# A fused encoder layer on one core: weight tiles 4608 bytes apart, norm tiles at the upper end of SBUF

## The chip, the cores and the metric

The kernel runs on one core of a Trainium2 chip. The metric is device time in microseconds (us) from one launch to its end. The kernel before took 1044.92 us (median of three runs, 1043.6 to 1045.78). One further execution was recorded by the hardware profiler; its rows are quoted below.

## The reference, cut to what matters

One layer of a streaming encoder on 1024 tokens of width 1024, float32 throughout:

```python
hn = _rmsnorm(h, norm_mix_g)
proj = einsum('bsd,de->bse', hn, w_in)          # 1024 x 2564 columns
# four token mixers on column groups: pooling, spatial gating, short convolution, Mamba-2 SSD
mix = concatenate([y_a, y_b, y_c, y_d], axis=-1)
h = h + einsum('bse,ed->bsd', mix, w_out)
hn = _rmsnorm(h, norm_ffn_g)
gate = silu(einsum('bsd,df->bsf', hn, w_gate))  # d_ff = 2816
up = einsum('bsd,df->bsf', hn, w_up)
h = h + einsum('bsf,fd->bsd', gate * up, w_down)
return _rmsnorm(h, final_norm_g)
```

## The kernel before

All arrays lie with 128 features (or 128 tokens) on the partitions. Every long product is taken in three matmuls: each operand `a` is split into a rounded part `hi` and a rest `lo` (`split`, L97 on ScalarE and L98 on VectorE; L101 and L102 where it is scaled as well), and `mm3` (L90 to L92) adds `hi*hi`, `hi*lo` and `lo*hi` in one PSUM bank. Each matmul is preceded by its own weight load, which in the profile runs on its own row (PEld) beside the matmul before it. The moving operand of nearly all of them is 512 columns of 4 bytes, that is 2048 bytes of each partition; the stationary one is 128 columns, 512 bytes.

The stages, in order of time:

- **Input projection and mixers (to about 276 us).** `proj_T` (L271) makes 14 tiles of 128 output features. For each of eight `k` it runs `hi*xh`, `hi*xl` and `lo*xh`, each for two halves of the tokens: six matmuls of 512 columns, 48 a tile, 672 in all. Stationary are the weight tiles `wh_t`/`wl_t` of the pool `whl`, moving the activations `x_hi`/`x_lo` of the pool `hl`. `proj_N` makes the z, u and v columns with the roles exchanged (256 or 260 columns moving). Between them run the short float32 matmuls of the state-space mixer and of the gating.
- **Output projection (to about 360 us).** `project`: 16 groups of 24 matmuls, stationary `oh`/`ol`, moving `mix_hi`/`mix_lo`.
- **First FFN block (to about 426 us).** `plain`: eight groups of 24.
- **Ten FFN chunks (426 to 1003 us).** Each runs `strassen` twice, for `w_gate` and `w_up`: seven products of 12 matmuls each (four `kt` by three). Stationary are the weight pairs `wg_i`/`wu_i` (pools `rfa` and `rf`, three slots in turn), moving the seven activation sets T[1] to T[7] (`t1h`, `t2h`, `t3h`, `t_hi`). Into their order the generator `down` puts the down projection of the chunk before: 84 matmuls a chunk, stationary `dh`/`dl`, moving the gated activations `x_ih`/`x_il`. So a chunk has 168 + 84 = 252 matmuls of 512 columns. VectorE makes all `lo` halves, adds the Strassen parts in PSUM to the sums (L734) and adds the down products to `h1` (L814).
- **Last block and final norm (from 1003 us).**

Where the tiles lie: pools take SBUF from its lower end upwards in the order in which they are opened, those with `side="right"` from its upper end downwards; a tile takes its bytes rounded up to 32. Offsets below are byte addresses in a partition, modulo 512:

| tiles | offset before |
|---|---|
| `hl` (x, mix and the sets T[4] to T[7]), `ext` (T[1], T[2]) | 0 |
| `wh`/`wl` of the input stage, slots 0 to 3 | wh 128, wl 256; wh 384, wl 0; the same again |
| `oh`/`ol`, FFN weight pairs, `t3h`/`t3l`, `x_ih`/`x_il`, `dh`/`dl` | 384 |
| working tiles `m` of `sml` (`g`, `u`, `xt`) | 96 |
| `wTs`, `pw`, `xbc`, `E`, `xb`, `xd` (short float32 products) | 128 |
| `rB`, `vnt`, `yzt`, `tri` | 0 |

The weight slots of the input stage are 1056 words of 4 bytes, 4224 bytes, apart, which is 8 times 512 and 128.

[...]

Of the kernel before, what the change touches and what calls it, by code (L numbers as in the profile page):

```python
# [9 lines left out]
F32 = mybir.dt.float32  # L10
# [5 lines left out]
P = 128  # L16
# [3 lines left out]
NB = S // P  # L20
# [3 lines left out]
NP = NF // 2 - 1  # L24
EPS = 1e-6
WK = 1040
WT = 1056
NH = 4


# [8 lines left out]
NPAR = C_INV + 32  # L39

R_LG, R_LB, R_DTB, R_ALOG, R_D = 0, 256, 512, 516, 520
NROW = 524
# [3 lines left out]
def encoder_kernel(ctx, tc, xT, w_t, w_z, w_vd, w_u, pool_w, sgu_wT, par, row, w_out, w_gate, w_up, w_dp, w_dl, gfin, out):  # L46
# [6 lines left out]
    acts = ctx.enter_context(tc.tile_pool(name="acts", bufs=8))  # L53


    const.tile([P, 8], F32, name="pad_left")
    padr = ctx.enter_context(tc.tile_pool(name="padr", bufs=1, side="right"))
    padr.tile([P, 24], F32, name="pad_right")

    gffn = const.tile([P, NK], F32, name="gffn")  # L60
    ident = const.tile([P, P], F32, name="ident")
# [9 lines left out]
    def rsqrt(pool, x, n, tag):  # L71

        y = pool.tile([P, n], F32, name=f"rs_y_{tag}", tag="rs_y", bufs=2)
        t = pool.tile([P, n], F32, name=f"rs_t_{tag}", tag="rs_t", bufs=2)
        yi, xi = y.bitcast(I32), x.bitcast(I32)
        V.tensor_scalar(out=yi, in0=xi, scalar1=1, scalar2=None, op0=ALU.arith_shift_right)
        V.tensor_scalar(out=yi, in0=yi, scalar1=-1.0, scalar2=float(0x5F3759DF), op0=ALU.mult, op1=ALU.add)
        for _ in range(3):
            V.tensor_tensor(out=t, in0=y, in1=y, op=ALU.mult)
            V.scalar_tensor_tensor(out=t, in0=t, scalar=-0.5, in1=x, op0=ALU.mult, op1=ALU.mult)  # L80
            V.scalar_tensor_tensor(out=y, in0=t, scalar=1.5, in1=y, op0=ALU.add, op1=ALU.mult)
        return y
# [27 lines left out]
    def inv_rms(pool, psp, tag, qs, name):  # L110

        n = qs[0].shape[1] // P
        ps = psp.tile([P, 512], F32, name=f"ps_ss_{name}", tag=tag)
        for b in range(n):
            for i, q in enumerate(qs):
                nc.tensor.matmul(ps[:, b:b + 1], q[:, b * P:(b + 1) * P], ones,
                                 start=(i == 0), stop=(i == len(qs) - 1))
        ms = pool.tile([P, n], F32, name=f"ms_{name}", tag="ms", bufs=2)
        V.tensor_scalar(out=ms, in0=ps[:, :n], scalar1=1.0 / D, scalar2=EPS, op0=ALU.mult, op1=ALU.add)
        return rsqrt(pool, ms, n, name)  # L120

    def rows_by_dma(pool, psp, tag, rn, n, out, name, rt=None, bufs=1):

        pt = psp.tile([P, 512], F32, name=f"ps_rt_{name}", tag=tag)
        nc.tensor.transpose(pt[0:n, 0:P], rn, ident)
        t = pool.tile([n, P], F32, name=f"rt_{name}", tag=rt or f"rt{n}", bufs=bufs)
        V.tensor_copy(out=t, in_=pt[0:n, 0:P])
        dr = tc.dram_tile([1, n * P], F32, name=f"rd_{name}")
        nc.sync.dma_start(out=dr.rearrange("o (b s) -> (o b) s", b=n), in_=t)
        nc.sync.dma_start(out=out, in_=dr.to_broadcast([P, n * P]))  # L130
# [21 lines left out]
    h1 = [None] * 8  # L152
# [22 lines left out]
    with ExitStack() as a:  # L175
        bt = a.enter_context(tc.tile_pool(name="bt", bufs=1, reuse_waits="tile"))
        sb = a.enter_context(tc.tile_pool(name="sb", bufs=1, reuse_waits="tile"))
# [3 lines left out]
        psm = a.enter_context(tc.tile_pool(name="psm", bufs=5, space=PSUM, reuse_waits="tile"))  # L181
        pss = a.enter_context(tc.tile_pool(name="pss", bufs=3, space=PSUM, reuse_waits="tile"))

        sb.tile([P, 16], F32, name="pad_sb")
        part = bt.tile([P, 128], F32, name="part")[:, :NPAR]
        nc.sync.dma_start(out=part, in_=par)

        def pc(c):
# [4 lines left out]
        def w_tiles(n, name):  # L193
            slot = next(loads) % 4
            raw = wraw.tile([P, WK], F32, name=f"wr_{name}", tag="wraw")[:, :n]
            hi = whl.tile([P, WT], F32R, name=f"wh_{name}", tag=f"whi{slot}")[:, :n]
            lo = whl.tile([P, WT], F32R, name=f"wl_{name}", tag=f"wlo{slot}")[:, :n]
            return raw, hi, lo
# [10 lines left out]
        rB = bt.tile([P, S], F32, name="rB")  # L209
# [10 lines left out]
        qa = [rB, yzt[:, 0:4, :].rearrange("p b c -> p (b c)")]  # L220
# [22 lines left out]
        for k in range(NK):  # L243
            x = mix[k]
# [3 lines left out]
                (V if k % 2 else nc.gpsimd).tensor_tensor(out=qa[k % 2], in0=qa[k % 2], in1=q, op=ALU.add)  # L248

        nc.gpsimd.tensor_copy(out=gffn, in_=part[:, C_GFFN:C_GFFN + NK])  # L250
        rowt = bt.tile([P, 544], F32, name="rowt")[:, :NROW]
        nc.sync.dma_start(out=rowt, in_=row.to_broadcast([P, NROW]))
        wTs = bt.tile([P, NH, P], F32, name="wTs")
        nc.sync.dma_start(out=wTs, in_=sgu_wT)
# [60 lines left out]
        rn = inv_rms(sb, pss, "sm", qa[:1], "x")  # L315
        for b in range(NB):
            ps = pv[b] if b < 2 else proj_N(wv, 260, b, "v", *((pss, "sm") if b % 2 else ()))
            if b == 3:
                rows_by_dma(sb, pss, "sm", rn, NB, rB, "x")
            V.scalar_tensor_tensor(out=dt[:, b, :], in0=ps[:, 256:260], scalar=rn[:, b:b + 1],  # L320
                                   in1=rowt[:, R_DTB:R_DTB + 4], op0=ALU.mult, op1=ALU.add)
            nc.scalar.mul(out=vn[b], in_=ps[:, :256], mul=rn[:, b:b + 1])
            st = sb.tile([P, 6], F32, name=f"st{b}", tag="st", bufs=2)
            V.bn_stats(out=st, in_=vn[b])
            V.bn_aggr(out=mv[:, b, :], in_=st)
# [67 lines left out]
        ss = sb.tile([P, NB * 2], F32, name="ss")  # L393
# [179 lines left out]

    ext = ctx.enter_context(tc.tile_pool(name="ext", bufs=1, reuse_waits="tile"))
    sml = ctx.enter_context(tc.tile_pool(name="sml", bufs=1, reuse_waits="tile"))
    sml.tile([P, 24], F32, name="pad_sml")
    NM = 6
    rfa = ctx.enter_context(tc.tile_pool(name="rfa", bufs=1, reuse_waits="tile"))
    fp = ctx.enter_context(tc.tile_pool(name="fp", bufs=8, space=PSUM, reuse_waits="tile"))
# [61 lines left out]
    with tc.tile_pool(name="ror", bufs=2, side="right", reuse_waits="tile") as ror, \  # L641
            tc.tile_pool(name="roh", bufs=1, side="right", reuse_waits="tile") as roh, \
            tc.tile_pool(name="ro", bufs=1, side="right", reuse_waits="tile") as ro, \
            tc.tile_pool(name="rol", bufs=1, side="right", reuse_waits="tile") as rol:
        wo, qa = {}, []

        def load_out(d):
            raw = ror.tile([P, S], F32, name=f"or{d}", tag="raw")
            nc.sync.dma_start(out=raw, in_=w_out[d])
            wo[d] = [(rol if d < 2 else roh if d < 4 else ro).tile([P, S], F32R, name=f"o{n}{d}") for n in "hl"]  # L650
            split(raw, *wo[d])

        w0 = {}
        pairs = [(w, i, j) for w, i in ((w_gate, 0), (w_up, 0), (w_gate, 1), (w_up, 1)) for j in range(2)]

        def first_w(m):
            w, i, j = pairs[m]
            src = ror.tile([P, S], F32, name=f"r0{m}", tag="raw")[:, :HS]
            nc.sync.dma_start(out=src, in_=w[i][:, j * HS:(j + 1) * HS])
            w0[m // 2, j] = w_pair(src, f"w0{m}")  # L660

        for th in range(2):
            qa.append(sums(f"h{th}"))
            for n in range(8):
                d = (n + 2 * th) % 8
                if th == 0 and n >= 2:
                    load_out(d)
                    residual(d)
                if th or n >= 2:
                    project(fp, "b", d, th, wo[d])  # L670
                last_add = squares(sml, d, n, th * HS, HS, qa[th])
                if th == 0 and n < 4:
                    mix_split(2 * n, 1)
                    mix_split(2 * n + 1, 1)
                if th == 0 and n >= 6:
                    load_out(n - 6)
                if th == 1 and n in (3, 4):
                    first_w(n - 3)
                if th == 1 and n == 1:
                    V.tensor_tensor(out=qa[0][0], in0=qa[0][0], in1=qa[0][1], op=ALU.add)  # L680
                    rn2 = inv_rms(sml, fp, "b", qa[0][:1], "h0")
                if th == 1 and n == 2:
                    rms_rows(rows_diag(sml, fp, "b", rn2, 4, "h0", "m", NM)[0], 0)
                    T[1], T[2] = t_set(0, "t1"), t_set(1, "t2")
                    for i in (1, 2):
                        for j in range(4):
                            t = sml.tile([P, HS], F32, name=f"n{i}{j}", tag="m", bufs=NM)
                            normed(4 * (i - 1) + j, 0, t)
                            split(t, *T[i][j])
# [174 lines left out]
    rn2 = []  # L864
    T[3], T[5], T[6] = t_set(2, "t3"), t_set(4, "t5"), t_set(5, "t6")

    def half_rms():
        follow(V.tensor_tensor(out=qa[1][0], in0=qa[1][0], in1=qa[1][1], op=ALU.add), last_add)
        rn2.append(inv_rms(sml, fp, "b", qa[1][:1], "h1"))

    rx2 = []

# [78 lines left out]
    for q in range(2):  # L951
        for i in range(2):
            wd[i, q] = w_pair(raw_tile(w_dl[i, :, q * HS:(q + 1) * HS], f"rl{i}{q}"), f"wl{i}{q}", tag=f"g{4 + 2 * i + q}" if i + q < 2 else None)
    ss = sml.tile([P, NB + 1], F32, name="ssf")
    ms = sml.tile([P, NB], F32, name="msf")
    LAST = NB - 1

    def square(b, c, to):
# [106 lines left out]
```

## Time and profile before

| | |
|---|---|
| median of three runs | 1044.92 us |
| the profiled execution, its own time | 1043.13 us |
| its span (first to last instruction) | 1041.4 us |
| PE (matmul) | 1019.9 us busy, 4836 instructions |
| PEld (weight loads) | 840.2 us |
| DVE (VectorE) | 828.7 us |
| ACT (ScalarE) | 399.2 us |
| POOL (GpSimd) | 293.2 us |
| granted TensorE clock, mean | 0.997 |

Matmuls overlap in the records: each one of 512 columns is shown for about 0.39 to 0.40 us, but the next one starts some 0.23 us after it. So the busy share of PE tells little, and the distance from one start to the next tells what a matmul costs. The timeline gives starts to 0.01 us; over ten or more matmuls that is 1 ns each.

### The profile page before, as it was taken

To read this page: it belongs to the slowest core of one execution; us is meant where nothing else is said; L and a number is where in the kernel's file an instruction comes from. 1 tells how busy PE (TensorE), PEld (TensorE's weight loads), DVE (VectorE), ACT (ScalarE), POOL (GpSimd) and SP (SyncE) were. 2 spreads that over 40 slices of the span, in tenths; PEclk is the share of its full clock that TensorE was granted. 3 is DMA by queue.
4 is the path that set the end of the run, shared out by engine and by line. 5 is a ranking of instruction groups with operands and counts; after the bars stand their busy time and mean duration, and the time that the engine had idled before them with its cause. 6 is when DMAs were issued, how large, how long until landed. Compare 5 with 4: busy or idle time off the path is not lost.

```text
span 1041.4 us, 13299 instructions
## 1 busy us (share of the span) xinstructions
PE 1019.9 (98%) x4836; PEld 840.2 (81%) x4836; DVE 828.7 (80%) x1375; ACT 399.2 (38%) x730; POOL 293.2 (28%) x325
## 2 busy tenths in 40 slices
PE   6999999999999999999999999999999999999997
PEld 5987998888887778888787878788787878788785
DVE  6698345887752689979898998979898898979777
ACT  8155412132440344434333343334333343434353
POOL 4014000000010140243444334443444334443302
PEclk9999999999999999999999999999999999999999
DMA  7311012111540201121111111121111111211203
GB/s 267 102 61 62 21 52 65 51 48 52 162 141 1 82 11 41 51 61 52 59 47 56 42 61 52 61 61 51 60 44 59 41 61 51 61 62 50 68 5 161
DMA packets 29682, 67.61 MB, mean 65 GB/s; under 512 B 3720, under 2 KB 4016, under 8 KB 29616
## 3 DMA queue, kind: packets, MB, share of 16 engines
q1 hardware_dynamic: 29616, 66.76, 19.6%
q8 instruction: 38, 0.62, 0.2%
q14 instruction: 28, 0.23, 0.1%
HBM read 62.53 MB, written 4.21 MB: 64 GB/s over the span
## 4 chain that ended last, share of the span: by engine, by line
PE 84%; DVE 12%; issue 2%; DMA 1%; ACT 1%; SPq 0%; POOLq 0%; DVEq 0%; ACTq 0%
PE pt L271 12%; DVE h L814 3%; PE po L90 3%; PE po L92 3%; PE po L91 3%; DVE dl L98 2%; PE p L90 2%; PE p L91 1%; DVE x_4l L98 1%; PE p L92 1%; DVE x_6l L98 1%; PE pn_u L91 1%; PE pn_v L91 1%; PE pn_z L90 1%; PE pn_z L92 1%
## 5 line engine op out<-in xcount | busy, mean ns | idle before, releaser
L800 POOL TENSOR_TENSOR rs<-rd 128x128 f32<-128x128 f32 x40 | 28.1, 701 | 220.5 <-DMA rd<-in_w_dp 167.0
L271 PE MATMUL pt<-x_hi,wh_t 128*128 128x512 f32 x224 | 73.6, 409 | 6.0 <-ACT wh_t L97 5.5
L271 PE MATMUL pt<-x_lo,wh_t 128*128 128x512 f32 x224 | 72.7, 402 | 1.5 <-DVE x_lo L102 1.5
L271 PE MATMUL pt<-x_hi,wl_t 128*128 128x512 f32 x224 | 72.7, 400 | 0.6 <-DVE wl_t L98 0.6
L98 DVE TENSOR_TENSOR dl<-rd,dh 128x256 fp32r<-128x256 f32 x80 | 57.7, 721 | 1.2 <-ACT dh L97 1.2
L271 PEld LDWEIGHTS pt<-x_hi,wh_t 128*128 128x128 f32 x224 | 42.7, 191 | 16.0 <-ACT wh_t L97 5.5
L271 PEld LDWEIGHTS pt<-x_lo,wh_t 128*128 128x128 f32 x224 | 42.3, 191 | 12.6 <-DVE x_lo L102 2.9
L271 PEld LDWEIGHTS pt<-x_hi,wl_t 128*128 128x128 f32 x224 | 42.3, 190 | 10.3 <-DVE wl_t L98 1.0
L924 ACT ACTIVATE g<-g 128x512 f32<-128x512 f32 x40 | 25.3, 633 | 62.7 <-DVE g L734 62.7
L97 ACT CAST dh<-rd 128x256 fp32r<-128x256 f32 x80 | 32.5, 406 | 41.9 <-PE pd92A L91 2.3
L90 PE MATMUL po<-mix_hi,oh 128*128 128x512 f32 x112 | 44.4, 396 | 0.0
L92 PE MATMUL po<-mix_hi,ol 128*128 128x512 f32 x112 | 44.2, 395 | 0.0
L91 PE MATMUL po<-mix_lo,oh 128*128 128x512 f32 x112 | 44.2, 395 | 0.0
L928 POOL TENSOR_TENSOR g<-g,u 128x512 f32<-128x512 f32 x20 | 29.7, 1483 | 35.0 <-DVE u L734 34.9
L97 ACT CAST dh<-rs 128x128 fp32r<-128x128 f32 (+1 forms) x80 | 28.0, 350 | 28.4 <-PE pd01A L91 2.2
L171 DVE TENSOR_TENSOR h<-po,h 128x512 f32<-128x512 f32 x16 | 11.0, 689 | 33.0 <-PE po L92 32.9
L98 DVE TENSOR_TENSOR wl_t<-wr_t,wh_t 128x1024 fp32r<-128x1024 f32 (+2 forms) x16 | 19.0, 1196 | 22.5 <-ACT wh_t L97 22.5
L608 POOL TENSOR_TENSOR qa_h<-qa_h,q 128x512 f32<-128x512 f32 x6 | 8.6, 1425 | 97.9 <-ACT q L607 97.9
L98 DVE TENSOR_TENSOR dl<-rs,dh 128x128 fp32r<-128x128 f32 (+1 forms) x80 | 33.6, 420 | 0.0
L742 POOL TENSOR_TENSOR s1g<-rg,rg 128x512 f32<-128x512 f32 x10 | 13.7, 1368 | 58.3 <-ACT x_1h L97 29.2
L98 DVE TENSOR_TENSOR wu_6l<-s1u,wu_6h 128x512 fp32r<-128x512 f32 x10 | 7.0, 698 | 27.5 <-ACT wu_6h L97 27.5
L709 POOL TENSOR_TENSOR rd<-rd 128x128 f32<-128x128 f32 x40 | 27.9, 696 | 0.0
(3167 smaller groups left out, 3418.8 us busy)
## 6 DMA issues: line engine op xcount, KB each, us to landing
rd<-in_w_dp SPq DMA_DIRECT2D x40, 256.0 KB, 2.6
rg<-in_w_gate SPq DMA_DIRECT2D x40, 256.0 KB, 2.7
ru<-in_w_up SPq DMA_DIRECT2D x40, 256.0 KB, 2.8
wr_t<-in_w_t SPq DMA_DIRECT2D x12, 512.0 KB, 3.3
or<-in_w_out SPq DMA_DIRECT2D x8, 512.0 KB, 4.7
h<-in_xT SPq DMA_DIRECT2D x8, 512.0 KB, 4.3
mix<-in_xT SPq DMA_DIRECT2D x7, 512.0 KB, 8.6
out<-hn SPq DMA_DIRECT2D x7, 512.0 KB, 2.6
```

The lines of the kernel that those rows point to most:

```text
L90: nc.tensor.matmul(ps, whi, xhi, start=start, stop=False, skip_group_check=skip)
L91: nc.tensor.matmul(ps, whi, xlo, start=False, stop=False, skip_group_check=skip)
L92: nc.tensor.matmul(ps, wlo, xhi, start=False, stop=stop, skip_group_check=skip)
L97: a = nc.scalar.copy(out=hi, in_=src)
L98: b = (eng or V).tensor_tensor(out=lo, in0=src, in1=hi.bitcast(F32), op=ALU.subtract)
L271: nc.tensor.matmul(ps[h], w1[:, ks], x1[k][:, h * HS:(h + 1) * HS], start=(k == 0 and first), stop=(k == NK - 1 and last))
L709: eng.tensor_tensor(out=out, in0=a_, in1=b_, op=ALU.subtract)
L742: G.tensor_tensor(out=s1, in0=a21, in1=a22, op=ALU.add)
L800: G.tensor_tensor(out=s1, in0=a21, in1=a22, op=ALU.add)
L814: V.tensor_tensor(out=t, in0=ps, in1=t, op=ALU.add)
L924: nc.scalar.activation(out=t, in_=t, func=AF.Silu)
L928: (V if i in (1, 2) else nc.gpsimd).tensor_tensor(out=g[i], in0=g[i], in1=t, op=ALU.mult)
```

## The change

Four edits, none of which touches an instruction's operation or order. (1) The distance of the input stage's weight tiles, `WT`, goes from 1056 to 1152 words: 4608 bytes, nine times 512. (2) The tiny tiles of the two later norms (`ms`, `rs_y`, `rs_t`, `ssf`, `msf`: 288 bytes with their rounding) leave the pool `sml` for a pool `tiny` at the upper end, whose pad grows from 24 to 48 words; the pad of `sml` (96 bytes) goes. (3) `part` and `rowt` lose their rounding up, and the pad of `sb` goes from 16 to 24 words. (4) The row of inverse norms, `rt_x` (512 bytes), shares the tile `jk`.

```diff
-WT = 1056
+WT = 1152
...
-    padr = ctx.enter_context(tc.tile_pool(name="padr", bufs=1, side="right"))
-    padr.tile([P, 24], F32, name="pad_right")
+    tiny = ctx.enter_context(tc.tile_pool(name="tiny", bufs=1, side="right"))
+    tiny.tile([P, 48], F32, name="pad_right")
...
-        sb.tile([P, 16], F32, name="pad_sb")
-        part = bt.tile([P, 128], F32, name="part")[:, :NPAR]
+        sb.tile([P, 24], F32, name="pad_sb")
+        part = bt.tile([P, NPAR], F32, name="part")
...
-        rowt = bt.tile([P, 544], F32, name="rowt")[:, :NROW]
+        rowt = bt.tile([P, NROW], F32, name="rowt")
...
-                rows_by_dma(sb, pss, "sm", rn, NB, rB, "x")
+                rows_by_dma(sb, pss, "sm", rn, NB, rB, "x", "jk")
...
-    sml.tile([P, 24], F32, name="pad_sml")
...
-                    rn2 = inv_rms(sml, fp, "b", qa[0][:1], "h0")
+                    rn2 = inv_rms(tiny, fp, "b", qa[0][:1], "h0")
...
-        rn2.append(inv_rms(sml, fp, "b", qa[1][:1], "h1"))
+        rn2.append(inv_rms(tiny, fp, "b", qa[1][:1], "h1"))
...
-    ss = sml.tile([P, NB + 1], F32, name="ssf")
-    ms = sml.tile([P, NB], F32, name="msf")
+    ss = tiny.tile([P, NB + 1], F32, name="ssf")
+    ms = tiny.tile([P, NB], F32, name="msf")
```

Worked out by the pool rule above: `sml` starts at 132608 as before and holds only its six working tiles, so all that lies above it (FFN weight pairs, `t3`, `x`, `dh`, `dl`, raw tiles) moves down by 288 + 96 = 384 bytes, from offset 384 to offset 0; the right pools (`oh`, `ol`) move down by 480 - 96 = 384 bytes, to offset 0. In the input stage `part` shrinks by 96, `rowt` by 64 and `sb` by 512 - 32, so the first weight tile moves from 163456 to 162816, which is 318 times 512, and its seven followers lie at offset 0 too. `rB`, `vnt`, `yzt` and `tri` come to offset 416, `wTs`, `pw` and `xbc` to 480, `E`, `xb` and `xd` to 0.

## Rows read from the trace of the kernel before

**Rows 1.** The page: engines (busy us, share of the span, instructions).

```profile
PE 1019.9 (98%) x4836; PEld 840.2 (81%) x4836; DVE 828.7 (80%) x1375; ACT 399.2 (38%) x730; POOL 293.2 (28%) x325
```

**Rows 2.** Engines by stage: stretch, length, busy us and count of each, clock, DMA.

```profile
161.00:276.00 115.00, 115.00 (x587) 95.36 (x586) 87.97 (x191) 31.65 (x67) 5.09 (x4) 1.00 0.20 65
276.00:338.00 62.00, 61.85 (x273) 49.68 (x271) 27.03 (x52) 17.64 (x26) 4.39 (x3) 1.00 0.28 94
...
426.00:1003.00 577.00, 574.85 (x2486) 465.13 (x2485) 511.43 (x795) 222.48 (x443) 232.47 (x244) 1.00 0.17 54
```

**Rows 3.** Timeline of PE, chunk 4, product 3 of w_up with down products (start us, shown us).

```profile
646.64 0.39 PE L90 MATMUL pu4E<-t3h,wu_3h 128*128 128x512 f32 x1
...
650.72 0.40 PE L91 MATMUL pg5A<-t1l,wg_1h 128*128 128x512 f32 x1
```

**Rows 4.** Timeline of PE, chunk 4, product 4 of w_up.

```profile
643.14 0.40 PE L92 MATMUL pu4B<-t_hi,wu_4l 128*128 128x512 f32 x1
643.38 0.39 PE L90 MATMUL pu4B<-t_hi,wu_4h 128*128 128x512 f32 x1
643.61 0.40 PE L91 MATMUL pu4B<-t_lo,wu_4h 128*128 128x512 f32 x1
...
645.48 0.40 PE L92 MATMUL pg5A<-t1h,wg_1l 128*128 128x512 f32 x1
```

**Rows 5.** Timeline of PE, chunk 4, product 7 of w_up.

```profile
636.71 0.39 PE L90 MATMUL pu4B<-t_hi,wu_7h 128*128 128x512 f32 x1
...
639.49 0.39 PE L90 MATMUL pd33A<-x_1h,dh 128*128 128x512 f32 x1
```

**Rows 6.** Timeline of PE, output projection, th 0.

```profile
296.11 0.40 PE L90 MATMUL po<-mix_hi,oh 128*128 128x512 f32 x1
...
302.42 0.39 PE L90 MATMUL po<-mix_hi,oh 128*128 128x512 f32 x1
```

**Rows 7.** Timeline of PE, input projection, weights in slot 0 (wh 128, wl 256).

```profile
220.63 0.64 PE L271 MATMUL pt<-x_hi,wh_t 128*128 128x512 f32 x2
221.11 0.63 PE L271 MATMUL pt<-x_lo,wh_t 128*128 128x512 f32 x2
...
222.03 0.64 PE L271 MATMUL pt<-x_hi,wh_t 128*128 128x512 f32 x2
```

**Rows 8.** The same, weights in slot 3 (wh 384, wl 0).

```profile
271.88 0.64 PE L271 MATMUL pt<-x_hi,wh_t 128*128 128x512 f32 x2
272.36 0.63 PE L271 MATMUL pt<-x_lo,wh_t 128*128 128x512 f32 x2
...
273.28 0.64 PE L271 MATMUL pt<-x_hi,wh_t 128*128 128x512 f32 x2
```

**Rows 9.** Timeline of PE, chunk 4, down products between products of w_up.

```profile
630.00 0.39 PE L91 MATMUL pd32A<-x_1l,dh 128*128 128x512 f32 x1
...
632.54 0.40 PE L90 MATMUL pu4A<-t_hi,wu_6h 128*128 128x512 f32 x1
```

**Rows 10.** Chain of waits: the second half of one VectorE split, chunks 1 and 9 (start, us).

```profile
490.98 1.71 DVE x_4l L98
...
960.47 1.71 DVE x_4l L98
```

**Rows 11.** Waits of PE, 380 to 1000 us (total us, times, longest).

```profile
PE pg7B L90 <- DVE g L734: 0.4, 1, 0.4
```

**Rows 12.** Timeline of DVE, chunks 3 and 4 (idle before, releaser).

```profile
591.23 0.69 DVE L814 TENSOR_TENSOR h<-pd22A,h 128x512 f32<-128x512 f32 x1 [0.22 <-PE pd22A L92]
...
612.75 0.68 DVE L734 TENSOR_TENSOR g<-g,pg4B 128x512 f32<-128x512 f32 x1
...
639.79 0.69 DVE L734 TENSOR_TENSOR u<-u,pu4B 128x512 f32<-128x512 f32 x1 [1.22 <-POOL rs L709]
```

**Rows 13.** Timeline of PE, z columns of `proj_N`.

```profile
124.08 0.28 PE L92 MATMUL pn_z<-wh_z,x_lo 128*128 128x256 f32 x1
...
125.88 0.29 PE L92 MATMUL pn_z<-wh_z,x_lo 128*128 128x256 f32 x1
```

## The prediction

> **What bounds the kernel now.** I read the page first: PE is shown busy for 1019.9 us, 98% of the span [rows 1]. VectorE has 828.7 us. [...] So the time is what the matmuls cost one after another, and the question is what sets the distance from one start to the next.
>
> The change adds no instruction and takes none away; it moves operands. What that can do must be read from matmuls that already lie differently today. There are three kinds of 512-column matmuls:
>
> - Moving and stationary operand both at offset 384 (products with `t3`, the down products): 18 starts in 4.08 us, 226.7 ns each [rows 3].
> - Moving at 0, stationary at 384 (six of seven Strassen products, the output projection, most of the first FFN block). Product 4: ten in 2.34 us, 234 ns [rows 4]. Product 7: twelve in 2.78 us, 231.7 ns [rows 5]. Output projection: 27 in 6.31 us, 233.7 ns [rows 6].
> - Input projection, moving at 0, stationary at 128 and 256, or at 384 and 0: six in 1.40 us, 233.3 ns [rows 7], and the same in the other pair of slots [rows 8].
>
> Two details speak for the offset of one operand against the other, and not for something else. First, product 4 steps 0.24 and 0.23 in turn [rows 4]: a rhythm of two, though the program repeats only after three matmuls. In the input projection the rhythm follows the weights instead: the two matmuls with a new `k` take 0.48 us, the next four 0.92 together, in both slots [rows 7, 8]. The moving operands are all at offset 0 there; what alternates is `wh` and `wl`. Second, both slots step alike, although one has 128 and 256 and the other 384 and 0: what they share is that `wh` is off by half of 256 bytes from the moving operand and `wl` is not. So I read the 5 to 7 ns as two read streams of PE, the 512 columns of one matmul and the 128 columns of the next weight load, that get in each other's way where their offsets differ, and settle at 226 to 227 ns where they agree. After the change all of them agree.
>
> Rows 7 and 8 also speak a little against it: a third of those weight loads do agree, modulo 256, and their pairs gain nothing. And the down products have equal offsets, but eleven of them in a row, right behind products of the other kind, take 2.54 us, 231 ns each [rows 9]. So the steps need a longer run of one kind to settle.
>
> **The change part by part.** The gain of a settled matmul is the distance of its kind less 226.7 ns. I take three quarters of it, because after each wait or short float32 matmul the settling starts again.
>
> - Input projection: the eight tiles from 161 us on are 384 matmuls of 233.3 ns; 384 x 6.6 x 0.75 = 1.9 us, all on the path, since PE has no idle time there. The six earlier tiles (288 matmuls, 1.4 us) lie beside VectorE's work and the first loads; I take half, 0.7. Together 2.6; ends 1.5 and 4.4 (672 x 6.6).
> - Output projection: 384 x (233.7 - 226.7) x 0.75 = 2.0 us; ends 1 and 2.7. First FFN block: eight groups of 24, a quarter of them with `t3` already; 0.9 us.
> - FFN chunks. One chunk lasts (960.47 - 490.98) / 8 = 58.69 us [rows 10] and has 252 matmuls of 512 columns; 0.3 to 0.4 us of it PE waits for VectorE [rows 11]. The rest is 58.3 us, 231.5 ns each. Settled it would be 57.1 us; three quarters of that is 0.9 us a chunk. But not all of this reaches the end. At 612.75 VectorE makes the `g` for which PE waits [rows 11, 12], and since 581.1 (639.79 less one chunk, where it last sat idle for long) it has had one gap of 0.22 us [rows 12]. Over those 31.6 us VectorE sets the pace, and whatever PE gains there turns into a longer wait at product 4 of `w_gate`. PE's gain counts over the other 27 us: 0.9 x 27 / 58.7 = 0.41, and the 0.22 us of slack on top: 0.63 us a chunk, 6.3 us over ten. Ends: 0, if VectorE takes all, and 12 us, if it takes nothing and the runs settle fully.
> - `proj_N`: fifteen matmuls of 256 columns take 1.80 us, 120.0 ns each [rows 13]. The settled 226.7 ns less 120.0 is 106.7 for 256 more columns, and 120.0 less 106.7 leaves the same 13.3 ns that a settled long matmul has beside its columns. They have nothing left to gain by this; I cost them at 0, and at 576 x 1 ns, 0.6 us, either way.
> - Short float32 matmuls in the input stage: some of their operands go to offset 480, which is 32 beside a multiple of 64, others to 0. No row shows them there. Some 300 matmuls by the 7 ns between rows 3 and 4 either way bound it at 2 us up or down; I take 0.
> - VectorE: the add at L814 works on `h1` at 0, the product at L734 on `g` at 96; they show 0.69 and 0.68 us [rows 12]. So offsets cost it nothing. The last tiles (`ssf`, `msf`, `ms`) change place only.
> [...]
>
> Sum: 2.6 + 2.0 + 0.9 + 6.3 = 11.8, say 12 us. The profiled execution took 1043.13 us, 1.8 less than the median shown; 1043.1 - 12 = 1031, and on the scale of the median 1033.
>
> [...]
>
> **The rivals.**
>
> - *VectorE takes nearly all of the FFN gain.* It is busy 511 of 577 us there [rows 2], and the gap-free stretch may reach further back than I read. Then 2.6 + 2.0 + 0.9 and some 1.5 us are left: 7 us, 1038.
> - *No change.* What is fast in rows 3 is something that stays: all fast moving tiles lie in the upper part of SBUF and all slow ones in the lower, and the change leaves them there. For it: the weights' slots with offsets 128/256 and 384/0 give the same time [rows 7, 8]. Against it: the step locked to the weights. Time 1044 to 1046.
> - *Slower: the moving operand alone decides, and 384 is its good place.* Then nothing gets faster, and the fast kinds lose. 240 products with `t3` go from 227 to 232 ns, 1.2 us; 840 down products from the 231 of rows 9 to 233, 1.7 us; 48 in the first block and 96 in the last, 0.7 us. That is 3.6 us on a PE without slack: 1048.5. It decides as soon as rows 3's kind, found again after the change, takes over 230 ns. For it: every matmul with its moving operand at 0 is slow today, whatever the weights' offset. Against it: the rhythm again, which a rule for the moving operand alone doesn't explain.
>
> **How the numbers follow.** My forecast has 0.46, VectorE taking the gain 0.18, no change 0.20, slower 0.16. A change of 0.2%, about 2 us, is what can be told from none. Faster: 0.46 + 0.18 = 0.64; same 0.20; slower 0.16. The likeliest time is 1033. If all runs settle and VectorE gives way, the gain is 4.4 + 2.7 + 1.2 + 12 = 20 us, 1024.5; that is the lower end. The upper end must take in the rival and most of "no change": 1046. The forecast's own range is 1027 to 1038.
>
> **What would show it.** Right: `t_hi` products, `po` and `pt` matmuls step at 226 to 228 ns in long runs, as product 3 does today; the wait at product 4 of `w_gate` grows from 0.4 us to about 0.7; a chunk takes about 58.0 us. Wrong: `pt` or `po` keep their 233 ns (then offsets don't matter), or product 3 rises to 232 (then the moving operand decides). If the steps fall and the chunk stays at 58.7 us with a longer wait, VectorE has it.

## The result, and the profile after

The changed kernel takes 1032.76 us (median of four executions, 1032.14 to 1033.78); the kernel before, beside it on the same chip, 1044.32 (1043.6 to 1045.78). The ratio is 0.9889, 95% interval 0.9871 to 0.9906: 11.6 us less, where 12 were forecast. The profiled execution after took 1033.78 us, span 1032.1.

In the kernel after all code lines stand one line lower (L90 to L92 are L91 to L93, L98 is L99, L271 is L272); L709, L734 and L814 keep their numbers. The page (busy us, share, instructions) and the windows by stage (length, busy us and count of PE, PEld, DVE, ACT, POOL, then clock, DMA share, GB/s), against [rows 1, 2]:

```profile
PE 1005.8 (97%) x4836; PEld 839.9 (81%) x4836; DVE 825.5 (80%) x1375; ACT 399.1 (39%) x730; POOL 292.3 (28%) x325
```

```profile
161.00:276.00 115.00, 115.00 (x602) 96.96 (x601) 88.93 (x196) 32.88 (x72) 5.17 (x4) 1.00 0.20 65
276.00:338.00 62.00, 60.74 (x273) 49.92 (x273) 28.17 (x53) 18.34 (x27) 4.73 (x4) 1.00 0.29 97
426.00:1003.00 577.00, 571.65 (x2540) 469.64 (x2539) 512.34 (x801) 228.30 (x455) 231.50 (x244) 1.00 0.18 54
```

The shares of busy time say almost nothing: 98% became 97%. The counts mislead: PE shows 2486 matmuls before and 2540 after in the 577 us, but the 54 more are short ones. After, the same window reaches further into the program, so it holds 64 of the short `ph` matmuls (transposes for the final norm) instead of 9. What the window does show is idle time, which rose from 2.15 to 5.35 us. What a matmul costs must be read from the steps.

The steps, from the timeline of PE (start us, shown us). First product 4 and product 7 of w_up in chunk 4, where the moving operand is `t_hi` or `t_lo`, against [rows 4, 5]; then product 3 with `t3`, against [rows 3]:

```profile
631.22 0.39 PE L91 MATMUL pu4B<-t_hi,wu_7h 128*128 128x512 f32 x1
...
633.94 0.39 PE L91 MATMUL pd33A<-x_1h,dh 128*128 128x512 f32 x1
...
637.12 0.39 PE L91 MATMUL pu4B<-t_hi,wu_4h 128*128 128x512 f32 x1
637.34 0.39 PE L92 MATMUL pu4B<-t_lo,wu_4h 128*128 128x512 f32 x1
637.57 0.39 PE L93 MATMUL pu4B<-t_hi,wu_4l 128*128 128x512 f32 x1
...
639.84 0.39 PE L93 MATMUL pg5A<-t1h,wg_1l 128*128 128x512 f32 x1
640.97 0.39 PE L91 MATMUL pu4E<-t3h,wu_3h 128*128 128x512 f32 x1
...
645.05 0.39 PE L92 MATMUL pg5A<-t1l,wg_1h 128*128 128x512 f32 x1
```

Twelve starts in 2.72 us (product 7), twelve in 2.72 us (product 4), eighteen in 4.08 us (product 3): 226.7 ns each. Product 7 came from 231.7, product 4 from 234 ns, and the rhythm of two in product 4 is gone; product 3 has not moved. The output projection and the last tile of the input projection, against [rows 6] and [rows 7, 8]:

```profile
296.24 0.39 PE L91 MATMUL po<-mix_hi,oh 128*128 128x512 f32 x1
...
302.36 0.39 PE L91 MATMUL po<-mix_hi,oh 128*128 128x512 f32 x1
```

```profile
268.81 0.62 PE L272 MATMUL pt<-x_hi,wl_t 128*128 128x512 f32 x2
269.26 0.62 PE L272 MATMUL pt<-x_hi,wh_t 128*128 128x512 f32 x2
269.72 0.61 PE L272 MATMUL pt<-x_lo,wh_t 128*128 128x512 f32 x2
...
273.34 0.62 PE L272 MATMUL pt<-x_hi,wh_t 128*128 128x512 f32 x2
```

27 starts in 6.12 us, 226.7 ns; 20 starts in 4.53 us, 226.5 ns, and no pair is 0.48 us any more. Each run of 17 or more matmuls of the input projection from 58 us on still begins with one to ten steps of 224 to 236 ns before it goes by 226 to 227; behind the nine waits at product 4 of `w_gate` the first step is 333 to 338 ns and the next two to nine are 224 to 236.

The chunk from the chain of waits (start, us), against [rows 10], and the wait at product 4 of `w_gate` (total us, times, longest), against [rows 11]:

```profile
486.98 1.55 DVE x_4l L99
...
951.27 1.64 DVE x_4l L99
```

```profile
PE pg7B L91 <- DVE g L734: 0.6, 1, 0.6
```

A chunk lasts (951.27 - 486.98) / 8 = 58.04 us instead of 58.69. PE now waits 0.5 or 0.6 us for VectorE in each of the nine chunks that have this wait.

Not foreseen was the clock. Windows of 4 us in the kernel before, the kernel after, and the kernel with all offsets at 480 (below); the windows that are not shown (88 and 338 us before, 382 us after) are at 1.00:

```profile
382.00:386.00 4.00, 4.00 (x10) 2.61 (x10) 4.00 (x7) 1.17 (x2) 3.26 (x3) 0.65 0.01 2
```

```profile
88.00:92.00 4.00, 4.00 (x14) 3.19 (x13) 3.90 (x4) 2.43 (x2) 1.88 (x4) 0.70 0.39 129
338.00:342.00 4.00, 4.00 (x12) 2.82 (x11) 2.73 (x5) 2.45 (x4) 0.91 (x1) 0.70 0.05 19
```

```profile
88.00:92.00 4.00, 4.00 (x19) 3.30 (x19) 3.90 (x3) 2.42 (x2) 1.75 (x4) 1.00 0.39 131
338.00:342.00 4.00, 4.00 (x19) 3.31 (x18) 4.00 (x8) 2.41 (x4) 0.00 (x0) 1.00 0.01 4
382.00:386.00 4.00, 4.00 (x20) 3.30 (x19) 4.00 (x7) 3.50 (x6) 0.00 (x0) 1.00 0.00 0
```

Behind some pauses of PE the granted clock fell from 1.00 to 0.50 for 3.4 us (in the kernel before, windows of 1 us from 383 us: 0.58, 0.50, 0.50, 0.71), and matmuls then stepped 426 to 427 ns. Before, this came behind the pause inside the first FFN block (0.65 over the 4 us); after, behind the pauses in the input stage and in the output projection (0.70 each), and not in the FFN block; at 480, behind none. Nine such steps from 338.5 us in the kernel after sum to 3.65 us; at 228 ns they would be 2.05: one dip costs 1.6 us. The profiled execution before loses one such dip and the one after two, so stages must be compared with the dips taken out. Executions of one kernel differ in this too: at 480 the profiled one had a mean clock of 0.998 and took 1030.77 us, the next two had 0.994 and took 1033.99 and 1033.3. (The fourth, 0.944 and 1034.2, fits neither; it was not profiled.)

Where the time of one execution came from, by the first matmul of each stage (start in the kernel before, and how much earlier it is after and at 480):

| first matmul of | before, us | after, earlier by | all at 480, earlier by |
|---|---|---|---|
| z columns | 105.16 | -1.75 | 0.04 |
| output projection | 274.68 | -0.02 | 1.77 |
| first FFN block | 368.15 | 0.64 | 4.06 |
| chunk 1 | 417.82 | 3.01 | 6.44 |
| last block | 1011.74 | 9.71 | 12.78 |

### The profile page after: what moved, and what is told of

It is laid out like the page before. It is cut to its first block, busy times and chain, and to the rows that moved or that the text cites. A ratio compares the mean times of both kernels' runs of the same rounds, so it can differ in the third digit from the quotient of the medians.

```text
span 1032.1 us, 13298 instructions
## 1 busy us (share of the span) xinstructions
PE 1005.8 (97%) x4836; PEld 839.9 (81%) x4836; DVE 825.5 (80%) x1375; ACT 399.1 (39%) x730; POOL 292.3 (28%) x325
## 4 chain that ended last, share of the span: by engine, by line
PE 83%; DVE 13%; issue 1%; DMA 1%; ACT 1%; SPq 0%; POOLq 0%; DVEq 0%; ACTq 0%
PE pt L272 12%; DVE h L814 3%; PE po L91 3%; PE po L92 3%; PE po L93 3%; DVE dl L99 2%; PE p L91 1%; PE p L92 1%; PE p L93 1%; DVE x_4l L99 1%; PE pn_u L92 1%; PE pn_v L92 1%; PE pn_z L92 1%; PE pn_z L93 1%; PE pn_v L93 1%
## 5 line engine op out<-in xcount | busy, mean ns | idle before, releaser
L272 PE MATMUL pt<-x_hi,wh_t 128*128 128x512 f32 x224 | 72.9, 405 | 6.2 <-ACT wh_t L98 5.7
L272 PE MATMUL pt<-x_lo,wh_t 128*128 128x512 f32 x224 | 72.1, 400 | 1.6 <-DVE x_lo L103 1.6
L272 PE MATMUL pt<-x_hi,wl_t 128*128 128x512 f32 x224 | 72.7, 400 | 0.5 <-DVE wl_t L99 0.5
L272 PEld LDWEIGHTS pt<-x_hi,wh_t 128*128 128x128 f32 x224 | 43.1, 193 | 15.8 <-ACT wh_t L98 5.7
L99 DVE TENSOR_TENSOR dl<-rd,dh 128x256 fp32r<-128x256 f32 x80 | 54.8, 685 | 1.1 <-ACT dh L98 1.1
L272 PEld LDWEIGHTS pt<-x_lo,wh_t 128*128 128x128 f32 x224 | 42.5, 191 | 11.7 <-DVE x_lo L103 2.9
L272 PEld LDWEIGHTS pt<-x_hi,wl_t 128*128 128x128 f32 x224 | 42.6, 192 | 9.5 <-DVE wl_t L99 0.9
L98 ACT CAST dh<-rd 128x256 fp32r<-128x256 f32 x80 | 32.5, 406 | 37.3 <-PE pd92A L92 2.3
L91 PE MATMUL po<-mix_hi,oh 128*128 128x512 f32 x112 | 44.3, 396 | 0.0
L93 PE MATMUL po<-mix_hi,ol 128*128 128x512 f32 x112 | 44.3, 396 | 0.0
L92 PE MATMUL po<-mix_lo,oh 128*128 128x512 f32 x112 | 44.3, 395 | 0.0
L98 ACT CAST dh<-rs 128x128 fp32r<-128x128 f32 (+1 forms) x80 | 28.0, 350 | 26.8 <-PE pd01A L92 1.4
L99 DVE TENSOR_TENSOR wl_t<-wr_t,wh_t 128x1024 fp32r<-128x1024 f32 (+2 forms) x16 | 19.0, 1195 | 22.9 <-ACT wh_t L98 22.9
L99 DVE TENSOR_TENSOR dl<-rs,dh 128x128 fp32r<-128x128 f32 (+1 forms) x80 | 33.4, 418 | 0.0
L742 POOL TENSOR_TENSOR s1g<-rg,rg 128x512 f32<-128x512 f32 x10 | 13.8, 1380 | 55.8 <-DMA rg<-in_w_gate 44.5
L99 DVE TENSOR_TENSOR wu_6l<-s1u,wu_6h 128x512 fp32r<-128x512 f32 x10 | 7.0, 700 | 27.6 <-ACT wu_6h L98 27.6
L709 POOL TENSOR_TENSOR rd<-rd 128x128 f32<-128x128 f32 x40 | 28.4, 709 | 0.0
```

The source lines that it names most:

```text
L91: nc.tensor.matmul(ps, whi, xhi, start=start, stop=False, skip_group_check=skip)
L92: nc.tensor.matmul(ps, whi, xlo, start=False, stop=False, skip_group_check=skip)
L93: nc.tensor.matmul(ps, wlo, xhi, start=False, stop=stop, skip_group_check=skip)
L98: a = nc.scalar.copy(out=hi, in_=src)
L99: b = (eng or V).tensor_tensor(out=lo, in0=src, in1=hi.bitcast(F32), op=ALU.subtract)
L272: nc.tensor.matmul(ps[h], w1[:, ks], x1[k][:, h * HS:(h + 1) * HS], start=(k == 0 and first), stop=(k == NK - 1 and last))
```

## The experiments

The theory: a matmul of 512 columns is slowed when the next weight load reads from another offset than the moving operand; only the difference of the two counts. Rivals: the absolute offset, the moving operand alone, the region of SBUF, and VectorE as what sets the chunk.

**All offsets at 480.** Every long operand lies at 480 modulo 512, so none is a multiple of 512 and all agree.

```diff
-    const.tile([P, 8], F32, name="pad_left")
...
-    tiny.tile([P, 48], F32, name="pad_right")
+    tiny.tile([P, 56], F32, name="pad_right")
```

> Every long TensorE operand of the changed kernel moved down by 32 bytes, so that moving and stationary lie at offset 480 modulo 512 and no longer at 0; nothing else changes. Theory (only the offset of one against the other counts): long runs step at 226.7 ns in every stage, time 1033 us within 2. Rival (a multiple of 512 is a good place in itself): steps of 231 to 234 ns, 1041 us or more.

1033.65 us (1030.77 to 1034.2), ratio 0.9891, interval 0.9877 to 0.9904: the same as the change. The timeline of the input projection:

```profile
217.10 0.62 PE L271 MATMUL pt<-x_hi,wh_t 128*128 128x512 f32 x2
...
221.18 0.62 PE L271 MATMUL pt<-x_hi,wh_t 128*128 128x512 f32 x2
```

18 starts in 4.08 us, 226.7 ns. So "multiples of 512" is not what helps; equality is. Since this execution has no dip, it is the cleanest to compare stages by.

**The input weights back.** The change, with the input stage's weights at 128/256/384/0 again.

```diff
-WT = 1152
+WT = 1056
...
-        sb.tile([P, 24], F32, name="pad_sb")
+        sb.tile([P, 56], F32, name="pad_sb")
```

> The changed kernel with the weight tiles of the input stage 4224 bytes apart again, at 128, 256, 384 and 0 as in the kernel before; output projection and FFN stay at 0. Theory: the input projection steps at 233 ns again (pairs 0.48, 0.46, 0.46 us), all later stages at 226.7; 1033 to 1036 us, because part of what the input stage gains is lost to a wait for VectorE and to the clock. Rival (weights' offsets don't matter): steps of 227 ns, 1032.8 us.

1033.98 us, ratio 0.9904 (0.989 to 0.9917); in the timeline of the input projection 18 starts take 4.20 us, 233.3 ns:

```profile
218.50 0.63 PE L272 MATMUL pt<-x_hi,wl_t 128*128 128x512 f32 x2
...
222.70 0.63 PE L272 MATMUL pt<-x_hi,wl_t 128*128 128x512 f32 x2
```

`x` lies where it lay in the change; moving the stationary operand alone brings the slow step back. All later stages keep 226.7, except the first two of the 16 groups of the output projection: their weights (`wh_o`, `wl_o`) lie in the slots of the input stage, and they step at 233.2 ns. The median can't tell 1.2 us more from none; the trace can: from the z columns to the output projection 0.03 us is gained, where the kernel at 480 gains 1.73.

**The input weights alone.** The kernel before with `WT = 1152`, the new `part`, `rowt` and pad of `sb`, and `rt_x` in `jk`; norm tiles and pad stay in `sml`. The edit, cut to its main line:

```diff
-WT = 1056
+WT = 1152
```

> The other half: weight tiles of the input stage 4608 bytes apart and at 0, but the norm tiles in sml and its pad back, so that output projection and FFN weights, t3, x, dh and dl lie at 384 as in the kernel before. Theory: input projection steps at 226.7 ns, output projection and FFN at 231 to 234 but for product 3 and runs of down products; 1042 to 1044.5 us, so that nearly all of the gain is the second half's. Rival (the input stage carries a third or more of it): 1040 us or less.

1042.62 us (median of eleven) beside 1044.86 for the kernel before, ratio 0.9988 (0.9979 to 0.9997). From the timeline of the input projection, 24 starts in 5.44 us, 226.7 ns:

```profile
216.24 0.62 PE L272 MATMUL pt<-x_lo,wh_t 128*128 128x512 f32 x2
...
221.68 0.62 PE L272 MATMUL pt<-x_lo,wh_t 128*128 128x512 f32 x2
```

The output projection starts 1.72 us earlier than before, close to the 1.77 at 480. Inside it the step changes with the weights' place. Its first two groups, with weights in the input slots (now at 0), and the groups after them, with `oh` at 384:

```profile
273.64 0.39 PE L91 MATMUL po<-mix_hi,wh_o 128*128 128x512 f32 x1
...
277.72 0.39 PE L93 MATMUL po<-mix_hi,wl_o 128*128 128x512 f32 x1
...
296.14 0.40 PE L91 MATMUL po<-mix_hi,oh 128*128 128x512 f32 x1
...
302.42 0.40 PE L91 MATMUL po<-mix_hi,oh 128*128 128x512 f32 x1
```

18 starts in 4.08 us, 226.7 ns; then 27 in 6.28 us, 232.6. With the input weights back it is the other way round: 233.2, then 226.7. The moving operand is `mix` at 0 throughout. The FFN's steps (230 to 233) stay slow but for product 3. The two kernels together reject the moving operand alone and the region: `x` and the weights are in the same part of SBUF in all four kernels.

**Scans of the difference.** The change, with the four weight slots shifted inside their 4608 bytes (`hi`, and `lo` in the same way); the moving operand stays at 0.

```diff
+OFF = (256, 64, 32, 192)      # second kernel: (16, 128, 384, 320)
+            o = OFF[slot] // 4
-            hi = whl.tile([P, WT], F32R, name=f"wh_{name}", tag=f"whi{slot}")[:, :n]
+            hi = whl.tile([P, WT], F32R, name=f"wh_{name}", tag=f"whi{slot}")[:, o:o + n]
...
```

> The changed kernel with hi and lo of each weight slot of the input stage moved inside their tiles: slot 0 (tiles t2, t6, t11, o0) to offset 256, slot 1 (t3, t7, t12, o1) to 64, slot 2 (t4, t8, t10) to 32, slot 3 (t5, t9, t13) to 192; x stays at 0. Read are the steps, not the time. Theory with a period of 256 bytes: slot 0 steps at 226.7 ns, the others at 230 to 234. With a period of 512: all four at 230 to 234. With 64: slots 0, 1 and 3 at 226.7 and slot 2 slow. With 32 or less: all at 226.7.

> The second scan of the input stage's weight offsets, x at 0: slot 0 at 16, slot 1 at 128, slot 2 at 384, slot 3 at 320, all else as in the changed kernel. The first scan gave 226.7 ns at 256, a cycle of 226, 229, 232 at 192, and 233 at 64 and 32. Theory (period 256 bytes): 384 repeats 128 to the nanosecond, at 231 to 234 ns, and 320 repeats 64 at 233.4; 16 lies between 32 and 0 and is slow, 230 or more. Rival (period 512, 256 being a second good place of its own): 384 and 128, 320 and 64 differ. The 256-column products of z and u have the same offsets with the roles exchanged: 113.5 ns at 192 and 118 at 64 were read, so 113.5 at none but 192 if the sign counts, and 118 again at 320.

1032.44 and 1033.65 us, one execution each. The timeline of the first, slot at 256 and slot at 64:

```profile
218.27 0.62 PE L274 MATMUL pt<-x_hi,wh_t 128*128 128x512 f32 x2
...
222.35 0.62 PE L274 MATMUL pt<-x_hi,wh_t 128*128 128x512 f32 x2
...
232.78 0.63 PE L274 MATMUL pt<-x_hi,wh_t 128*128 128x512 f32 x2
...
236.98 0.39 PE L274 MATMUL pt<-x_hi,wh_t 128*128 128x512 f32 x1
```

256: 18 starts in 4.08 us, 226.7 ns, like 0. 64: 18 in 4.20 us, 233.3. 192 (from 260.95 us): 12 in 2.74 us, 228.3 (229 over the whole run), a little below the 230 to 234 expected; 32: 233. `wh` and `wl` of a slot moved together here, so it is not the distance of one weight tile from the other that counts. The second scan, slot at 16, twice in one and the same tile:

```profile
218.74 0.62 PE L274 MATMUL pt<-x_hi,wh_t 128*128 128x512 f32 x2
...
222.82 0.39 PE L274 MATMUL pt<-x_hi,wh_t 128*128 128x512 f32 x1
...
226.43 0.63 PE L274 MATMUL pt<-x_hi,wh_t 128*128 128x512 f32 x2
...
229.69 0.63 PE L274 MATMUL pt<-x_lo,wh_t 128*128 128x512 f32 x2
```

18 starts in 4.08 us, 226.7 ns; then, behind some 2.7 us of short matmuls, 14 in 3.26 us, 233. So at 16, which was expected to be slow, the same offsets give either step, and a run keeps the one it fell into. 128 and 384 show one and the same rhythm of seven (228 to 241 ns, mean 232), 320 shows that of 64 (231 and 236 in turn, or 233). So of the differences tried those 256 bytes apart step alike (0 and 256 at 226.7 ns, 128 and 384 at 232, 64 and 320 at 233). In the input projection equal offsets settled at 226 to 227 ns in every run of 17 or more matmuls of the kernel after, and of the other differences tried only 16 settled there, sometimes.

**VectorE relieved, after and before.** Both kernels without the second add of each down step (that add of the `B` bank is left out of the computation).

```diff
         product(2, B, True)
-        add(dp, 0, B)
```

> The changed kernel without one of the seven adds (0.68 us each) of each down step, the one of product 2; the output lacks that part. Theory (VectorE sets the pace over about 30 us of each chunk, and part of PE's gain turns into the wait at product 4 of w_gate): the wait of 0.6 us goes, a chunk falls from 58.04 to 57.2 to 57.5 us, time 1026 to 1028. Rival (the wait is there anyway, VectorE's load decides nothing): chunk 57.9 to 58.1, 1032 or more.

> The kernel before with the same add left out. Theory: its smaller wait of 0.4 us goes, a chunk falls from 58.69 to about 58.3, 1040 to 1042; so the two kernels without the add differ by 0.9 to 1.1 us a chunk, where they differ by 0.65 with it. Rival: 58.7 and 0.65.

1025.99 us after (ratio 0.9823, 0.9808 to 0.9838), 1040.81 before (0.9959, 0.9945 to 0.9974). First matmul of chunks 2 and 10 in the timelines of after and before without the add:

```profile
462.40 0.39 PE L91 MATMUL pg2A<-t1h,wg_1h 128*128 128x512 f32 x1
...
921.20 0.39 PE L91 MATMUL pg10A<-t1h,wg_1h 128*128 128x512 f32 x1
```

```profile
468.58 0.40 PE L90 MATMUL pg2A<-t1h,wg_1h 128*128 128x512 f32 x1
...
934.16 0.40 PE L90 MATMUL pg10A<-t1h,wg_1h 128*128 128x512 f32 x1
```

458.80 / 8 = 57.35 and 465.58 / 8 = 58.20 us a chunk. With VectorE relieved the change is worth 0.85 us a chunk and 14.8 us in all; with VectorE as it is, 0.65 and 11.6. In the kernel after a wait of 0.3 us at product 4 is left even so in chunks 4, 6 and 10. In chunks 7 and 8 PE waits in neither kernel: 57.12 and 58.16 us a chunk, a gain of 1.04. So VectorE takes between a quarter and two fifths of the FFN gain.

**One subtraction on GpSimd.** The change, and the last subtraction of `g_split`, which VectorE did in each chunk, moved.

```diff
-        minus(V, g21, g21, t2)
+        minus(nc.gpsimd, g21, g21, t2)
```

> The changed kernel with the last subtraction of g_split (0.95 us on VectorE, ahead of x_4) on GpSimd; nothing left out. If VectorE's queue alone sets the pace, a chunk loses most of the 0.6 us wait: 57.5 us, 1027 to 1029. Rival (GpSimd takes 1.4 us or more for it and holds VectorE up while both read SBUF, or x_4h comes late): 58.0 us a chunk or more, 1032.5 and above.

1025.98 us (1025.51 to 1027.24), ratio 0.9824 (0.981 to 0.9839): 6.8 us below the change and 18.5 below the kernel before beside it (1044.51). That is also below the 1027 to 1029 expected. Its waits of PE for VectorE from 426 us on, all of them, and its chunks in the timeline:

```profile
PE pg8B L91 <- DVE g L734: 0.3, 1, 0.3
PE pg10B L91 <- DVE g L734: 0.3, 1, 0.3
PE pg6B L91 <- DVE g L734: 0.3, 1, 0.3
```

```profile
460.96 0.39 PE L91 MATMUL pg2A<-t1h,wg_1h 128*128 128x512 f32 x1
...
919.31 0.39 PE L91 MATMUL pg10A<-t1h,wg_1h 128*128 128x512 f32 x1
```

458.35 / 8 = 57.29 us; 252 settled matmuls would be 57.13. The subtraction, 0.95 us on VectorE and 1.74 on GpSimd, took 0.75 us off each chunk: VectorE's stretch ahead of product 4 was on the path.

It did so in part by way of another instruction. Behind the subtraction VectorE makes the split `x_4l`. Its shortest, median and longest duration (ns) in the kernel after and in this one:

```profile
L99 DVE TENSOR_TENSOR x_4l<-g,x_4h x10: 682/1778/1781, 427.5 to 951.2; 128x512 fp32r<-128x512 f32 x10
L99 DVE TENSOR_TENSOR x_4l<-g,x_4h x10: 676/679/1781, 426.1 to 942.3; 128x512 fp32r<-128x512 f32 x10
```

In the traces before, after, without the add and with this edit it shows 1.78 us where a GpSimd sum of two weight blocks (L709 or L742) had begun 0.05 to 0.22 us earlier, and 0.68 us where none ran or it began later (at less than 0.08 us ahead either comes out). After, that is so in nine chunks of ten. Here it is so in chunks 6, 8 and 10, and without the add, after the change, in 4, 6 and 10: the very chunks whose wait is left. So much of what both edits gave is this one split at 0.68 instead of 1.78 us, with no GpSimd sum begun just ahead of it. No run moved the split by itself.

**More in the same direction.** z and u weight tiles at 192 bytes in the change; that with the subtraction on GpSimd; and that with a second subtraction there.

```diff
+            o = 48 if n == 256 else 0
...
-        minus(V, g12, g22, g12)
+        minus(nc.gpsimd, g12, g22, g12)
```

> The kernel after, with the 256-column weight tiles of z and u moved 192 bytes up inside their slots. In the scan, 256-column matmuls whose moving operand lay 192 bytes beside the stationary one stepped 113 to 114 ns, against 120.0 where both agree. There are 384 of them. If this is a property of the offset: pn_z and pn_u step 113.5 ns, 384 x 6.5 ns = 2.5 us less between the first z matmul and t6, of which all reaches the output projection, since nothing waits there: 1030.3 us. Rival: they settle at another rhythm at that offset and stay at 118 to 120 ns: 1032.8 us, as after.

> The kernel after, with the z and u tiles at 192 bytes and with the last subtraction of g_split on GpSimd. The two edits act in different stages, so their gains should add: 1026.0 us of the kernel with the subtraction alone less 2.5 us, 1023.5 us; chunk 57.3 us. Rival: the z and u columns keep 120 ns: 1026.0 us.

> As the kernel with both edits, and the subtraction for product 7 (g12 = g22 - g12) on GpSimd too. With one subtraction moved a chunk takes 57.29 us; 252 settled matmuls are 252 x 226.7 = 57.1 us. If the 0.3 us waits for VectorE at product 4 of w_gate that are left in some chunks are all that remains: chunk 57.15 us, another 1.0 to 1.5 us less, 1022.3 us. Rival: GpSimd is too late with product 7's operand, PE waits for it in the down products: chunk above 57.3 us, 1024 us or more.

1031.2 (1030.78 to 1034.04), 1027.87 (1025.03 to 1029.02) and 1030.28 us (1029.42 to 1032.05): all three above what was expected (1030.3, 1023.5 and 1022.3). The 256-column matmuls fell from 120.0 to 117.7 ns in z, and in u to 113.3 in some runs of matmuls and 117.7 in others, two steps at one offset; from the first z matmul to the next tile of the input projection this gave 1.05 us, not 2.5, and no median shows it. The second subtraction did harm: the chunk goes back from 57.35 to 57.81 us. The first step of product 4 of `w_gate` is 0.49 to 0.75 us in all eight chunks from 2 to 9, where with one subtraction moved it is above 0.3 us in three, and PE now waits in chunks 2, 5 and 8 (0.2 to 0.3 us each) for the adds of the down products to free a bank, which it doesn't do with one subtraction moved. The kernel with one subtraction on GpSimd stays the best.

## Why the prediction was right

**The step.** The reading that the difference of the two offsets sets the step held for matmuls of 512 columns: equal offsets settle at 226.7 ns at 0, at 480 and at a difference of 256, and moving the weights alone undoes the gain or brings it. It is not a complete rule. At a difference of 16 some runs were as fast, and 256 columns did better at a difference of 192 (113.3 to 117.7 ns, against 120.0). Why the matmuls beside `wl`, which agreed modulo 256 before, gained nothing then stays open too. Two of the three rivals fall: "no change" (1044 to 1046) by the result, and its ground, the region of SBUF, by the input weights alone; "slower" (1048.5) by product 3, which kept its 226.7. That the streams of the moving operand and of the weight load are what collides is the author's reading and not shown: no run took a weight load away. What is shown is the step: with the input weights back, `wh` lies 128 bytes beside `x` modulo 256 and `wl` 0, and a matmul costs 233.3 ns, 6.6 more than 226.7.

**The size of each term**, by the execution at 480, which has no dip:

- Input projection 2.6: measured 1.8. The eight tiles from 161 us on gave 1.81 us (predicted 1.9; 4.7 of 6.6 ns per matmul, so three quarters was right). The 0.7 us of the earlier tiles never came. PE only waited longer for VectorE's `da`; the waits of PE before and after (at 480 it is 2.1 as well):

```profile
PE ps_acs L365 <- DVE da L358: 1.0, 1, 1.0
```

```profile
PE ps_acs L366 <- DVE da L359: 2.1, 1, 2.1
```

- Output projection 2.0: measured 2.29 (4.06 - 1.77), 6.0 ns of 7.0.
- First FFN block 0.9: it shows 2.38, of which about 1.6 is the dip that the kernel before had there; 0.7 to 0.8 is left.
- FFN chunks 6.3: 6.34 at 480 (12.78 - 6.44) and 6.70 in the profiled execution after. Both halves hold: with VectorE relieved 0.85 to 1.04 us a chunk (predicted 0.9), with it as it is 0.65 (0.63). Not seen was that 1.1 us of VectorE's gap-free stretch was the split `x_4l`, at 1.78 instead of 0.68 us beside a GpSimd sum. The wait grew from 0.2 to 0.4 us to 0.5 to 0.6, not quite the 0.7 named. The rival in which VectorE takes nearly all of the gain overrated a real effect.
- `proj_N` 0: its step is 120 ns as before, and from z to the next tile of the input projection 0.08 us is lost. The number is right, its reason is not: 120.0 was said to leave nothing to gain, and at other offsets these matmuls take 117.7 and 113.3 ns. The short float32 matmuls were not measured by themselves; the stages that hold them leave no more than a few tenths unexplained.

Sum at 480, up to the last block: 12.8 us in the trace, 11.2 without the dip of before, against 11.8. In the profiled execution after, two dips of its own against one of before's make 9.7. Behind that, 0.4 to 0.5 us is lost again in both (the spans differ by 12.3 and 9.3). The medians, over executions with and without dips on both sides, give 11.6. That the difference of the offsets sets the step and that most of the terms were right is shown; that the sum came within half a microsecond is in part luck, with dips of 1.6 us each on either side and one term 0.8 us too high.

**What was missed.** Not one term, but a noise of 1.6 us each in three places: whether the clock falls behind a pause. It was visible before (0.65 at 382 us) and not looked at, since the windows by stage average it away. The gain of the early tiles should have been costed at 0 for the reason used in the FFN: VectorE's result sets when the next matmul may start (PE waited 2.1 us for `da` instead of 1.0).

## What to carry to other kernels

When PE has no idle time, measure start to start by kind of operand, not busy time; here 5 to 7 ns of 232 to 234 hid in where tiles lie. Matmuls of 512 columns of 4 bytes settled at 226.7 ns where the moving operand and the weights loaded beside it lay at equal offsets modulo 256 bytes (both at 0, 384 or 480, or 256 apart), and went at 229 to 234 at most other differences, so equal offsets are the first thing to try; for 256 columns they were not the best here (120.0 ns, against 113.3 and 117.7 at a difference of 192). Then look for the engine that takes over: here a single subtraction per chunk (0.95 us), moved from VectorE to GpSimd, was worth another 6.8 us, and a second one moved the same way gave some of that back.

## What the runs showed of the hardware that was not expected

- For 512 columns differences 256 bytes apart gave the same step: 0 and 256 gave 226.7 ns, 128 and 384 about 232, 64 and 320 about 233; 32 gave 233 and 192 gave 229.
- At an unequal difference a run fell into one of several rhythms and kept it: 226.7 or 233 ns at 16 within one tile, 117.7 or 113.3 ns for 256 columns at 192. For 256 columns equality was not the best: 120.0 ns, against 113.3 to 118 at 64 and 192.
- Settling at equal offsets took up to ten matmuls: one to ten steps of 224 to 236 ns at the start of a run of the input projection, two to nine behind the first step after the waits at product 4 of `w_gate`.
- The same pauses of PE (1.3 us at 334 to 338 us, 2.1 us at 86) dropped the granted clock from 1.00 to 0.50 in one trace and not in another, at about 1.6 us a time. What decides it stays open.
- A VectorE split of 128x512 took 1.78 instead of 0.68 us where a GpSimd sum had begun 0.05 to 0.22 us before it (one split per FFN chunk, nine of ten in the kernel after).
